# A hybrid attention and HGRN layer on one core: p·w_pp at the front, two column blocks in seven half-size products, their sums built during the first value columns

## The chip, the cores and the metric

The kernel runs on one core of a Trainium2 chip. The metric is the device time of one execution in microseconds (us); lower is better. TensorE (PE) does the matmuls, and PEld stands for its weight loads. VectorE (DVE), ScalarE (ACT) and GpSimd (POOL) work on tiles in the on-chip memories SBUF and PSUM. SyncE (SP) issues nearly all transfers, in the order in which they stand in its queue.

## The reference

x is 1024 tokens by 2048. What is computed, cut to the products that matter here:

```
u = rmsnorm(x, g_pre)
z = u @ w_in                   # 2048 x 9216; columns: attention q k v gate (1024 each),
                               # HGRN q, f_fwd, f_bwd, v, gate (1024 each)
y = [attention(q,k,v) * silu(gate) | rmsnorm(hgrn(q,f,v)) * silu(gate)]
h = x + rmsnorm(y @ w_out, g_post)          # 2048 x 2048
e = p @ w_pp                                # p 1024 x 256, w_pp 256 x 2048
out = h + rmsnorm(sigmoid(h @ w_pg) * e, g_ple)
```

All of it is float32.

## The kernel before

Each float32 product is made of three matmuls. The activations are split into a high part (fp32r) and a low part (bf16), the weights likewise: `uh` and `ul` hold the two parts of u transposed, for two halves of 512 tokens. A weight piece of 256 KB (`piece`, L69 to L85) is loaded as `raw` by SP; ACT casts it to `wh` (L82), POOL subtracts to get `wl` (L83), and DVE casts it to `wb` (L84). The matmuls are hi·wh, hi·wl and lo·wb. Each of the four kinds of tile has 3 buffers, so a piece's cast waits until the piece three back has been used. PSUM has 8 banks of 128x512: four with tag `gb`, four with tag `wk`.

The program goes through these stages; a scheduler orders the instructions of each engine.

1. `prenorm` (L155) loads x in eight tiles of 128 tokens (1 MB each), squares and scales them, transposes them on PE (`xp`, L171) and splits them into `uh` and `ul`. The first 512 attention value columns (`v_group(0, ...)`, L729) are computed in three passes over the 16 pieces of their weights: for tokens of tiles 0 and 1, of 2 and 3, and of 4 to 7, each as soon as those tiles are normalised. In a pass with two tiles a piece feeds 6 matmuls and every second `wl` is made by DVE; with four tiles it feeds 12.
2. `v_group(1)`, `(2)` and `(3)`: the other attention value columns (2560) and the HGRN value columns (7168, 7680), all eight token tiles at once, 24 matmuls of 512 columns for a piece.
3. Eight HGRN heads (`hgrn`, L229). Each has four products of 128 columns (`group`, L93: 96 matmuls of 512 columns): forward gate, backward gate, q, and the output gate (L376, columns 8192 on). The first `group` of the next head, and this head's own last one, are interleaved with the head's small matmuls: the scan's `pl` and `pa`, the state update `pu` (L366), the output `pout` (L385 to L389) and the last transposes `po` (L405).
4. Eight attention head pairs, then `y_phase` for either half of the tokens (y·w_out), then `g_phase(0)` and `g_phase(1)` (h·w_pg). p·w_pp is computed inside `g_phase` by `e_phase`, which uses `gemm` on the `wk` banks (tile `pe`, L810, L811, L814), for both halves 96 matmuls; its result goes to `G`, where the gate multiplies it.

Of the kernel before, what the change touches and what calls it, by code (L numbers as in the profile page):

```python
# [705 lines left out]
def tile_hybrid(ctx, tc, x, p, positions, w_in, w_out, g_pre, g_post, g_hg, lb_fwd, lb_bwd, w_pg, w_pp, g_ple, out):  # L706
# [22 lines left out]
    def v_group(cg, toks, pool):  # L729
        c0 = (2048, 2560, 7168, 7680)[cg]  # L730
        pb = {t: (K.gb() if t < NGB else K.wk("vb")) for t in toks}
        for k in range(KT):
            wh, wl, wb = K.piece(w_in[128 * k:128 * k + 128, c0:c0 + 512], [512], prio=False,
                                 sub=V if len(toks) == 2 and k % 2 else None)
            for t in toks:
                hi = K.uh[t // 4][:, k, 128 * (t % 4):128 * (t % 4) + 128]
                nc.tensor.matmul(pb[t], hi, wh, start=(k == 0), stop=False)  # L737
                nc.tensor.matmul(pb[t], hi, wl, start=False, stop=False)  # L738
            for t in toks:
                lo = K.ul[t // 4][:, k, 128 * (t % 4):128 * (t % 4) + 128]  # L740
                nc.tensor.matmul(pb[t], lo, wb, start=False, stop=(k == KT - 1))
        for t in toks:
            vo = pool.tile([128, 512], F32, name="vo", tag="vo", bufs=3)
            (nc.scalar.copy if t % 2 else V.tensor_copy)(vo, pb[t])
            nc.sync.dma_start(vD[cg][128 * t:128 * t + 128, :], vo)

    with tc.tile_pool(name="p0", bufs=1) as p0:
        warm = K.sp.tile([128, 1], F32, name="warm", bufs=1)
        V.memset(warm, 1.0)
        nc.scalar.activation(warm, warm, AF.Sqrt)  # L750
        K.prenorm(x2, g_pre, p0, (0, 1))
        v_group(0, (0, 1), p0)
        K.prenorm(x2, g_pre, p0, (2, 3))
        v_group(0, (2, 3), p0)
        late = K.prenorm(x2, g_pre, p0, (4, 5, 6, 7))
        v_group(0, (4, 5, 6, 7), p0)
        with tc.issue_after(late[0].ins), tc.issue_after(late[1].ins):
            K.hg_consts((lb_fwd, lb_bwd), g_hg)
        for cg in range(1, 4):
            v_group(cg, tuple(range(8)), p0)  # L760
    with tc.tile_pool(name="big", bufs=1) as big:
        K.big = big
        for h in range(8):
            K.hgrn(w_in, h, vD[2 + h // 4][:, 128 * (h % 4):128 * (h % 4) + 128], yD[8 + h])
            if h == 0:
                with tc.issue_after(late[0].ins), tc.issue_after(late[1].ins):
                    K.att_consts(positions)
        for hp in range(8):
            K.att(w_in, hp, vD[hp // 4][:, 128 * (hp % 4):128 * (hp % 4) + 128], yD[hp])
    fin = ctx.enter_context(tc.tile_pool(name="fin", bufs=1))  # L770
    Y = [fin.tile([128, 4, D], F32, name=f"Y{i}", tag=f"Y{i}") for i in range(2)]
    yss = [fin.tile([128, 4, 4], F32, name=f"yss{i}") for i in range(2)]
    gss = [fin.tile([128, 4, 4], F32, name=f"gss{i}") for i in range(2)]
    korder = list(range(8, 16)) + list(range(8))

    def s2(name):
        return fin.tile([128, 512], F32, name=name, tag="s2", bufs=3)

    def g2(src, cs):
# [161 lines left out]
    def every3(f, ext={}, off=0):  # L941
        def hook(cg, j, k=None):
# [3 lines left out]
            if n in ext:  # L946
                ext[n]()
# [80 lines left out]
```

## Time and profile before

| | us |
|---|---|
| median of 3 runs | 2906.36 (2903.96 to 2910.01) |
| the profiled execution | 2911.69 |
| its span, first to last instruction | 2909.9 |
| PE busy | 2785.7 (96%) |
| DVE busy | 1508.4 (52%) |
| POOL busy | 1023.8 (35%) |
| mean granted clock of TensorE | 0.992 |

The span is what the trace covers; 1.8 us of the profiled execution lie around it. A busy share is an average over stages that have different limits, so the stages are to be read one by one: where PE is busy through a stage, only fewer or shorter matmuls shorten it; where it isn't, some other engine or a transfer ends last there. The trace lacks some matmul records.

### The profile page before, as it was taken

The page shows a single profiled execution, that of the slowest core. Times are in us where ns is not written, and L with a number is a line of the kernel's source. Part 1 is how long each engine was busy: PE and PEld are TensorE (multiplying, and loading weights), DVE is VectorE, ACT ScalarE, POOL GpSimd, SP SyncE. Part 2 cuts the span into 40 slices and gives each one's busy share as a digit, 9 for nine tenths or more (in the row PEclk, how much of TensorE's full clock was granted, in tenths as well). Part 3 has the DMA queues.
Part 4 walks back from the last instruction along what each step waited for, and adds up shares of the span by engine and source line. Part 5 has one row for each costly group of instructions (what it writes and reads, how often), then busy time and mean ns, then how long its engine had stood idle before and what let it go on. Part 6 is the DMA issues. An engine that isn't in the chain of part 4 may idle for free. (4 is left out here: it accounts for less than half of the span.)

```text
span 2909.9 us, 46582 instructions
## 1 busy us (share of the span) xinstructions
PE 2785.7 (96%) x18128; PEld 1885.7 (65%) x18384; DVE 1508.4 (52%) x2833; ACT 925.5 (32%) x1672; POOL 1023.8 (35%) x769
## 2 busy tenths in 40 slices
PE   6999999999999999999999999999999899999997
PEld 4666666676667676676666666666566566665664
DVE  8601116856346346356655555555755645555555
ACT  5311112222122112124434444443533223333323
POOL 2422223413313313322222222222244554666555
PEclk9999999999999999999999999999999999999998
DMA  6412221211111111121221222122344543433453
GB/s 226 121 55 80 77 86 39 66 52 39 57 52 44 52 52 45 51 65 55 78 70 45 73 76 71 47 74 71 113 122 133 159 142 97 131 113 109 146 155 106
DMA packets 251614, 250.54 MB, mean 86 GB/s; under 512 B 21633, under 2 KB 175233, under 8 KB 250241
## 3 DMA queue, kind: packets, MB, share of 16 engines
q1 hardware_dynamic: 242224, 238.62, 27.6%
q10 hardware_dynamic: 9168, 8.93, 0.9%
q8 instruction: 144, 2.36, 0.3%
q14 instruction: 78, 0.63, 0.1%
HBM read 205.54 MB, written 29.36 MB: 81 GB/s over the span
## 5 line engine op out<-in xcount | busy, mean ns | idle before, releaser
L83 POOL TENSOR_TENSOR wl<-raw,wh 128x512 fp32r<-128x512 f32 x568 | 764.7, 1350 | 1599.8 <-ACT wh L82 1507.1
L84 DVE CAST wb<-raw 128x512 bf16<-128x512 f32 x584 | 430.5, 740 | 785.2 <-PE gb L106 281.8
L82 ACT CAST wh<-raw 128x512 fp32r<-128x512 f32 x584 | 358.4, 617 | 1241.7 <-PE gb L101 414.7
L101 PE MATMUL gb<-uh,wh 128*128 128x512 f32 x1792 | 744.3, 415 | 0.0
L102 PE MATMUL gb<-uh,wl 128*128 128x512 f32 x1792 | 708.6, 395 | 0.0
L106 PE MATMUL gb<-ul,wb 128*128 128x512 bf16 x1632 | 405.7, 380 | 9.8 <-issue 1.8
L101 PEld LDWEIGHTS gb<-uh,wh 128*128 128x128 f32 x1792 | 337.1, 188 | 82.9 <-issue 1.2
L102 PEld LDWEIGHTS gb<-uh,wl 128*128 128x128 f32 x1792 | 337.1, 188 | 68.9 <-issue 1.0
L106 PEld LDWEIGHTS <-wb 128*128 128x128 bf16 x1792 | 158.4, 98 | 204.6 <-issue 54.3
L810 PE MATMUL gb<-wh,yh 128*128 128x512 f32 x512 | 231.2, 452 | 2.8 <-DVE Y L842 2.8
L810 PE MATMUL gb<-wh,th 128*128 128x512 f32 x480 | 215.8, 450 | 0.0
L811 PE MATMUL gb<-wl,yh 128*128 128x512 f32 x512 | 203.7, 398 | 4.7 <-POOL wl L83 4.7
L811 PE MATMUL gb<-wl,th 128*128 128x512 f32 x480 | 190.6, 397 | 5.4 <-POOL wl L83 5.4
L645 DVE CUSTOM_DVE_ANT_1 asm<-asc,amask 128x512 f32<-128x512 f32 x128 | 88.3, 690 | 119.9 <-PE asc L639 119.7
L814 PE MATMUL gb<-wb,yl 128*128 128x512 bf16 x479 | 133.7, 383 | 1.6
L814 PE MATMUL gb<-wb,tl 128*128 128x512 bf16 x452 | 126.2, 384 | 1.0
L650 ACT ACTIVATE asm<-asm,anm 128x512 f32<-128x512 f32 x128 | 92.5, 722 | 90.3 <-DVE anm L648 90.0
L810 PEld LDWEIGHTS gb<-wh,yh 128*128 128x128 f32 x512 | 97.6, 191 | 33.3 <-DVE Y L842 3.3
L737 PE MATMUL gb<-wh,uh 128*128 128x512 f32 x256 | 116.4, 461 | 1.4 <-ACT wh L82 1.3
L811 PEld LDWEIGHTS gb<-wl,yh 128*128 128x128 f32 x512 | 97.4, 190 | 24.3 <-POOL wl L83 5.9
L738 PE MATMUL gb<-wl,uh 128*128 128x512 f32 x256 | 102.4, 407 | 10.9 <-POOL wl L83 7.9
L634 PE MATMUL asc<-ak,aqt 128*32 128x256 bf16 x1536 | 109.7, 401 | 3.2 <-issue 2.4
(274 smaller groups left out, 3668.4 us busy)
## 6 DMA issues: line engine op xcount, KB each, us to landing
raw<-in_w_in_dram SPq DMA_DIRECT2D x320, 256.0 KB
raw<-in_w_out_dram SPq DMA_DIRECT2D x128, 256.0 KB
raw<-in_w_pg_dram SPq DMA_DIRECT2D x128, 256.0 KB
xt<-in_x_dram SPq DMA_DIRECT2D x8, 1024.0 KB
vD<-vo SPq DMA_DIRECT2D x32, 256.0 KB
raw<-yD SPq DMA_DIRECT2D x32, 256.0 KB
xr<-in_x_dram SPq DMA_DIRECT2D x32, 256.0 KB
ak<-ak SPq DMA_DIRECT2D x96, 64.0 KB
```

Of the source, the lines that this page charges most:

```text
L82: nc.scalar.copy(wh, raw)
L83: (sub or nc.gpsimd).tensor_tensor(wl, raw, f32(wh), op=ALU.subtract)
L84: nc.vector.tensor_copy(wb, raw)
L101: nc.tensor.matmul(pb[hf], wh[:, k], self.uh[hf][:, kt], start=(kt == 0), stop=False)
L102: nc.tensor.matmul(pb[hf], wl[:, k], self.uh[hf][:, kt], start=False, stop=False)
L106: mm = nc.tensor.matmul(pb[hf], wb[:, k], self.ul[hf][:, kt], start=False, stop=(kt == KT - 1))
L634: t = nc.tensor.matmul(sc[32 * r:32 * r + 32, :256], qb[:, sq, 32 * r:32 * r + 32], KS[s][:, h, r::4], start=(s == 0), stop=False, skip_gr ...
L737: nc.tensor.matmul(pb[t], hi, wh, start=(k == 0), stop=False)
L738: nc.tensor.matmul(pb[t], hi, wl, start=False, stop=False)
L810: nc.tensor.matmul(pb[t], a, pc[0], start=first, stop=False)
L811: nc.tensor.matmul(pb[t], a, pc[1], start=False, stop=False)
L814: nc.tensor.matmul(pb[t], lo[:, k, 128 * t:128 * t + 128], pc[2], start=False, stop=last)
```

## The change

**p·w_pp.** `e_product(0)` and `e_product(1)` compute it at the head of the program, ahead of `prenorm`: per half 1 load of p, 8 transposes, 8 pieces of w_pp, 96 matmuls. The result leaves PSUM through 16 tiles `eo` a half and is stored to DRAM (`eD`, 32 transfers of 256 KB for both). `g_phase` loads it back (`e_load`, 4 transfers of 1 MB a half). The `e_phase` of the end and the hooks around it are gone. `xt` has 4 buffers in place of 5.

**Two column blocks.** The HGRN value columns (1024 of them) and the HGRN output gate of all heads (1024) are each computed by a `Block`: the 2048 rows and the 1024 columns of the weights are halved, the activations too, and the block takes seven products of half-size operands in place of eight. Each product has 8 pieces of 12 matmuls, so a block has 672 matmuls where `v_group(2)` and `(3)`, or the eight gate groups, had 768. Four of the weight operands are sums: T2, T1, T3 and T4 are formed by DVE from `raw`, `rb` and `TB` before they are split. Four of the activation operands are sums too, loaded from DRAM (`rh`, `rl`, 8 loads of both a block). The results are combined on ACT and DVE. The gate's are multiplied by their sigmoid and stored to `zD`, and each head loads its 512 KB into `hgt` in place of its fourth `group`.

**The activation sums.** `s_build`, called 8 times, makes four sums for each of 8 row tiles: 12 DVE instructions and 4 ACT casts a call, and 8 stores (`sh`, `sl`; 12.6 MB in all).

```diff
+    def e_product(hf, pool, stage):
+        src = pool.tile([128, 4, PLE], F32, name="pr", tag="pr", bufs=2)
+        nc.sync.dma_start(src, pin[512 * hf:512 * hf + 512, :].rearrange("(t p) c -> p t c", p=128))
...
+        for cg in range(4):
+            def sink(t, p):
+                eo = stage.tile([128, 512], F32, name="eo", tag="tA", bufs=4)
+                (V.tensor_copy if t % 2 else nc.scalar.copy)(eo, p)
+                nc.sync.dma_start(eD[hf][128 * t:128 * t + 128, chunk(cg)], eo)
+            gemm(w_pp, (eh, el), [0, 1], 512 * cg, sink, 2, K.gb)
...
+    def s_build(pool, kk):
...
+        add(x1, a21, l21)
+        add(x2, a22, l22)
+        add(x0, a11, l11)
+        add(x2, x1, x2)
+        s2 = x("sx3")
+        sub(s2, x2, x0)
+        sub(x1, x0, x1)
+        sub(x0, a12, s2)
+        add(x0, x0, l12)
+        for i, t in enumerate((x2, s2, x1, x0)):
...
+            nc.scalar.copy(h, t)
+            sub(l, t, f32(h))
+            nc.sync.dma_start(sD[i][0][:, kk], f32(h))
+            nc.sync.dma_start(sD[i][1][:, kk], l)
...
+        def weights(self, name, kk):
...
+            elif name == "T2":
+                t = self.raw(kk, 0, 1)
+                sub(t, t, self.raw(kk, 0, 0, True))
+                d = self.TB[:, kk]
+                sub(d, self.raw(kk, 1, 1, True), t)
+                t = d
+            elif name == "T1":
+                t = self.raw(kk, 1, 1)
+                sub(t, t, self.TB[:, kk])
+            elif name == "T3":
+                t = self.raw(kk, 1, 1)
+                sub(t, t, self.raw(kk, 0, 1, True))
...
+            nc.scalar.copy(wh, t)
+            sub(wl, t, f32(wh), nc.gpsimd)
+            V.tensor_copy(wb, t)
...
+        def run(self):
...
+            self.product(0, orig(0, 0), "11", True)
...
+            self.product(1, orig(0, 1), "21", True)
...
+            self.product(0, comb(1), "T2", False)
...
+            self.product(1, comb(0), "T1", True)
...
+            self.product(0, comb(2), "T3", False)
...
+            self.product(1, comb(3), "22", False)
...
+            self.product(0, orig(1, 1), "T4", False)
...
+            e_product(0, p0a, p0)
+            e_product(1, p0a, p0)
             K.prenorm(x2, g_pre, p0a, (0, 1))
...
+        v_group(1, tuple(range(8)), p0)
+        with tc.tile_pool(name="p0s", bufs=1) as p0s:
+            for kk in range(8):
+                s_build(p0s, kk)
...
+            Block((7168, 7680), False, v_out(2), p0, False).run()
+            Block((8192, 8704), True, z_out("hg", p0), p0, True).run()
...
-        self.group(w_in, base + 4096, lambda hf, p: self.gate_evac(gt[:, 512 * hf:512 * hf + 512], p))
+        nc.sync.dma_start(gt, self.zD["hg"][h])
...
     def g_phase(hf, G, hook, fin_t=None, get=None, tail=1):
+        e_load(hf, G)
         for cg in range(4):
-            if cg < 2:
-                e_phase(hf, G, 2 * cg)
-                e_phase(hf, G, 2 * cg + 1)
```

The scheduler places the new instructions. On SP, whose queue issues the loads, this is the start of the program (L75 is the load of a weight piece, L159 that of an x tile):

```order
+L75 DMA raw<-in_w_pp_dram 128x512 x3
+L769 DMA pr<-in_p_dram 128x4x256 x2
 L159 DMA xt<-in_x_dram 128x2048
+L75 DMA raw<-in_w_pp_dram 128x512 x3
 L162 DMA gpre<-in_g_pre_dram 128x2048
+L781 DMA eD_102<-eo 128x512 x2
 L159 DMA xt<-in_x_dram 128x2048
-L75 DMA raw<-in_w_in_dram 128x512 x3
-L159 DMA xt<-in_x_dram 128x2048 x2
-L75 DMA raw<-in_w_in_dram 128x512 x3
-L159 DMA xt<-in_x_dram 128x2048 x2
+L75 DMA raw<-in_w_pp_dram 128x512 x2
```

The first loads of w_pp and of p, and the first stores `eD`, now stand between the loads of x.

On DVE, in the third pass of `v_group(0)` (tokens 512 to 1023), the casts `wb` (L84) stood one behind the other before:

```order
L422 TENSOR_SCALAR am<-aj_3970 128x1
L465 SCALAR_TENSOR_TENSOR ainv<-am,ainv 128x1
L84 CAST wb<-raw 128x512 x13
L744 COPY vo<-vb 128x512 x2
L84 CAST wb<-raw 128x512 x16
L744 COPY vo<-gb 128x512 x2
```

Now four instructions of `s_build` (tiles `sx_...`, `sxl`; L808 is `add` and L811 is `sub` of the changed kernel) stand between one cast and the next, here for two casts in the middle of that pass:

```order
L84 CAST wb<-raw 128x512
L808 TENSOR_TENSOR sx_2363<-uh_94,ul_96 128x512
L808 TENSOR_TENSOR sx_2365<-sx_2364,sx_2365 128x512
L808 TENSOR_TENSOR sx_2400<-uh_95,ul_97 128x512
L811 TENSOR_TENSOR sx_2370<-sx_2365,sx_2363 128x512
L84 CAST wb<-raw 128x512
L811 TENSOR_TENSOR sx_2364<-sx_2363,sx_2364 128x512
L811 TENSOR_TENSOR sxl<-sx_2365,sxh 128x512
L811 TENSOR_TENSOR sx_2363<-uh_94,sx_2370 128x512
L811 TENSOR_TENSOR sxl<-sx_2370,sxh 128x512
L84 CAST wb<-raw 128x512
```

In all 61 of the 96 instructions of `s_build` stand in the third pass of `v_group(0)`, and 35 between the first five casts of `v_group(1)`.

On PE, within a head, this is what stood before between the last state update `pu` and the first output `pout` (29 matmuls of a `group`, L101, L102, L106; a few rows of them):

```order
L106 MATMUL gb<-ul_96,wb 128x512
L366 MATMUL pu<-hvt,hk_3699 128x128 x7
L106 LDWEIGHTS wb
L106 MATMUL gb<-ul_96,wb 128x512
...
L101 MATMUL gb<-uh_94,wh 128x512
L102 MATMUL gb<-uh_94,wl 128x512
...
L106 MATMUL gb<-ul_97,wb 128x512
L385 MATMUL pout<-hvt,ATT 128x128
L389 MATMUL pout<-hst,Q_3364 128x128
```

And now, with the same names:

```order
L106 MATMUL gb<-ul_96,wb 128x512
L366 MATMUL pu<-hvt,hk_6099 128x128 x7
L385 MATMUL pout<-hvt,ATT 128x128
L106 LDWEIGHTS wb
L106 MATMUL gb<-ul_96,wb 128x512
...
L106 MATMUL gb<-ul_97,wb 128x512
L101 MATMUL gb<-uh_94,wh 128x512
L102 MATMUL gb<-uh_94,wl 128x512
L385 MATMUL pout<-hvt,ATT 128x128
L387 MATMUL pout<-hst,Q_5764 128x128
```

Seven matmuls of a `group` (that of the next head's forward gate) stand between `pu` and the bulk of `pout` where 29 stood. Behind `pout`, ahead of `po`, 22 stand where 96 stood.

## Rows read from the trace of the kernel before

**Rows 1.** The page, its head and part 1: span, then busy time, share of the span and instructions of each engine.

```profile
span 2909.9 us, 46582 instructions
...
PE 2785.7 (96%) x18128; PEld 1885.7 (65%) x18384; DVE 1508.4 (52%) x2833; ACT 925.5 (32%) x1672; POOL 1023.8 (35%) x769
```

**Rows 2.** Busy time by stage, over the whole span. Columns: the stretch (us from the start), its length, busy us (and instructions) of PE, PEld, DVE, ACT and POOL, the granted clock, the mean busy share of the 16 DMA engines, GB/s. The stretches are: x and the first two passes of `v_group(0)`; its third pass; `v_group(1)` to `(3)`; the heads; then, behind the attention pairs and the two `y_phase` that are left out, `g_phase(0)` with `g_phase(1)` as far as the last `pe` matmul, and the rest of `g_phase(1)`.

```profile
0.00:98.40 98.40, 69.51 (x315) 44.93 (x320) 78.63 (x138) 55.13 (x94) 33.12 (x28) 0.97 0.61 206
98.40:141.90 43.50, 43.40 (x188) 28.64 (x191) 24.54 (x78) 11.90 (x21) 19.31 (x15) 1.00 0.38 92
141.90:401.40 259.50, 258.71 (x1135) 177.40 (x1154) 28.44 (x60) 36.27 (x60) 61.68 (x49) 1.00 0.24 70
401.40:1268.00 866.60, 836.17 (x7581) 601.59 (x7668) 462.37 (x902) 188.09 (x307) 256.63 (x197) 1.00 0.18 53
...
2457.40:2755.00 297.60, 279.88 (x1206) 179.81 (x1229) 166.85 (x207) 104.74 (x202) 180.14 (x132) 0.98 0.40 121
2755.00:2910.00 155.00, 135.21 (x564) 86.46 (x573) 84.87 (x123) 44.91 (x85) 86.85 (x62) 0.94 0.43 133
```

**Rows 3.** POOL in order of time, in the third pass of `v_group(0)` and then in `v_group(1)`. Columns here and in the other rows in order of time: start, us of the entry, engine, line, operation, out<-in, count, and in brackets the idle time before it with what ended it.

```profile
120.36 1.29 POOL L83 TENSOR_TENSOR wl<-raw,wh 128x512 fp32r<-128x512 f32 x1 [1.43 <-ACT wh L82]
123.09 1.29 POOL L83 TENSOR_TENSOR wl<-raw,wh 128x512 fp32r<-128x512 f32 x1 [1.43 <-ACT wh L82]
...
152.15 1.26 POOL L83 TENSOR_TENSOR wl<-raw,wh 128x512 fp32r<-128x512 f32 x1 [3.91 <-ACT wh L82]
157.54 1.26 POOL L83 TENSOR_TENSOR wl<-raw,wh 128x512 fp32r<-128x512 f32 x1 [4.13 <-ACT wh L82]
```

**Rows 4.** DVE in order of time: a cast `wb` in the third pass of `v_group(0)`, the end of that pass, and a cast in `v_group(1)`.

```profile
123.46 1.21 DVE L84 CAST wb<-raw 128x512 bf16<-128x512 f32 x1 [1.52 <-PE vb L738]
...
141.90 1.29 DVE L744 COPY vo<-vb 128x512 f32<-128x512 f32 x2 [0.87 <-PE vb L741]
...
153.38 0.43 DVE L84 CAST wb<-raw 128x512 bf16<-128x512 f32 x1 [4.86 <-PE vb L741]
```

**Rows 5.** The front. DVE's first scaling of an x tile; PE's first transposes and its first product.

```profile
9.06 2.35 DVE L167 SCALAR_TENSOR_TENSOR xt<-xt,xr,gpre 128x2048 f32<-128x2048 f32 x1
...
11.56 3.65 PE L171 MATMUL xp<-ident,xt 128*128 128x128 f32 x16 [11.56 <-DVE xt L167]
16.49 0.79 PE L737 MATMUL gb<-wh,uh 128*128 128x512 f32 x1 [1.28 <-ACT wh L82]
```

**Rows 6.** What the transfers reach: columns as in group 2, for three 5 us pieces of the front, one stretch at the start of the heads and one of `g_phase(1)`.

```profile
5.00:10.00 5.00, 0.00 (x0) 0.00 (x0) 1.89 (x7) 2.21 (x3) 0.00 (x0) 1.00 0.98 415
20.00:25.00 5.00, 3.86 (x24) 2.72 (x23) 3.65 (x6) 3.15 (x6) 0.00 (x0) 1.00 0.87 298
30.00:35.00 5.00, 3.28 (x18) 2.02 (x16) 4.69 (x12) 4.47 (x9) 1.68 (x2) 1.00 0.94 313
402.00:410.00 8.00, 7.95 (x36) 5.84 (x36) 1.91 (x4) 2.38 (x4) 1.27 (x1) 1.00 0.78 270
2700.00:2735.00 35.00, 34.89 (x153) 23.24 (x155) 18.51 (x18) 8.03 (x13) 16.50 (x13) 1.00 0.51 159
```

**Rows 7.** DVE and POOL in order of time within a head: DVE's product of two SBUF tiles (`Q`, two of 128x512 in an entry) without and with POOL's `wl` beside it, and that `wl`.

```profile
693.08 1.29 DVE L281 TENSOR_TENSOR Q<-Q,TB 128x512 f32<-128x512 f32 x2
...
698.70 2.03 DVE L281 TENSOR_TENSOR Q<-Q,TB 128x512 f32<-128x512 f32 x2
...
697.64 1.94 POOL L83 TENSOR_TENSOR wl<-raw,wh 128x512 fp32r<-128x512 f32 x1 [6.37 <-ACT wh L82]
```

**Rows 8.** The end of a head, in order of time: PE's last `pu` entry, the first and last `pout`, and `po`; then DVE's last state update `hst` and the normalised output `hon`.

```profile
712.58 1.83 PE L366 MATMUL pu<-hvt,hk 128*128 128x128 f32 x14 [1.12 <-DVE hk L352]
...
720.74 0.38 PE L385 MATMUL pout<-hvt,ATT 128*128 128x128 f32 x2
...
725.42 0.39 PE L387 MATMUL pout<-hst,Q 128*128 128x128 f32 x2
...
747.22 1.04 PE L405 MATMUL po<-ident,hon 128*128 128x128 f32 x8
...
715.87 1.49 DVE L372 SCALAR_TENSOR_TENSOR hst<-hst,TB,pu 128x128 f32<-128x128 f32 x4
...
729.71 1.29 DVE L398 TENSOR_TENSOR hon<-pout,hr 128x512 f32<-128x512 f32 x2
```

**Rows 9.** The `pe` work (p·w_pp) at the end. First PE in the four stretches that hold it: length, PE busy, clock, DMA share, GB/s, of which the first, the third and the sum are shown. Then the first of the three matmuls of the tile `pe` (count, ns min/median/max, first and last start), and two PE entries in order of time with the wait before them.

```profile
2457.40:2472.00 14.60, 13.43 (x56) 1.00 0.25 74
...
2678.00:2697.00 19.00, 14.84 (x55) 0.91 0.47 139
...
sum 64.00, PE 53.95; mean PE 13.49
...
L810 PE MATMUL pe<-wh,eh x64: 388/584/988, 2457.5 to 2753.5; 128*128 128x512 f32 x64
...
2690.16 0.71 PE L810 MATMUL pe<-wh,eh 128*128 128x512 f32 x1 [3.18 <-DVE G L900]
...
2750.11 0.50 PE L810 MATMUL pe<-wh,eh 128*128 128x512 f32 x1 [1.91 <-DVE G L900]
```

**Rows 10.** DVE's last scalings, two SBUF tiles in, beside POOL's work at the end (count, ns min/median/max).

```profile
L990 DVE SCALAR_TENSOR_TENSOR G<-G,gr,Y x12: 746/1248/1792, 2882.5 to 2904.3; 128x512 f32<-128x512 f32 x12
```

More of the change, by code (lines that the diff above doesn't have):

```diff
@@ L727, in tile_hybrid @@
     vD = [K.dr.tile([S, 512], F32, name=f"vD{i}") for i in range(4)]
[L729 to L779, printed above, removed]
-        t = fin.tile([128, 512], F32, name="g2", tag="g2", bufs=2)
-        nc.sync.dma_start(t, src[0:1, cs].to_broadcast([128, 512]))
-        return t
@@ new lines, in v_group @@
+    def v_group(cg, toks, pool):
+        c0 = (2048, 2560, 7168, 7680)[cg]
+        pb = {t: (K.gb() if t < NGB else K.wk("vb")) for t in toks}
+        for k in range(KT):
+            wh, wl, wb = K.piece(w_in[128 * k:128 * k + 128, c0:c0 + 512], [512], prio=False,
+                                 sub=V if len(toks) == 2 and k % 2 else None)
+            for t in toks:
+                hi = K.uh[t // 4][:, k, 128 * (t % 4):128 * (t % 4) + 128]
+                nc.tensor.matmul(pb[t], hi, wh, start=(k == 0), stop=False)
+                nc.tensor.matmul(pb[t], hi, wl, start=False, stop=False)
+            for t in toks:
+                lo = K.ul[t // 4][:, k, 128 * (t % 4):128 * (t % 4) + 128]
+                nc.tensor.matmul(pb[t], lo, wb, start=False, stop=(k == KT - 1))
+        for t in toks:
+            vo = pool.tile([128, 512], F32, name="vo", tag="tA", bufs=4)
+            (nc.scalar.copy if t % 2 else V.tensor_copy)(vo, pb[t])
+            nc.sync.dma_start(vD[cg][128 * t:128 * t + 128, :], vo)
@@ new lines, in tile_hybrid @@
+    K.zD = zD
+    with tc.tile_pool(name="big", bufs=1) as big:
+        K.big = big
+        for h in range(8):
+            K.hgrn(w_in, h, vD[2 + h // 4][:, 128 * (h % 4):128 * (h % 4) + 128], yD[8 + h])
+            if h == 0:
+                with tc.issue_after(late[0].ins), tc.issue_after(late[1].ins):
+                    K.att_consts(positions)
+        for hp in range(8):
+            K.att(w_in, hp, vD[hp // 4][:, 128 * (hp % 4):128 * (hp % 4) + 128], yD[hp])
+    fin = ctx.enter_context(tc.tile_pool(name="fin", bufs=1))
@@ L945, in hook @@
                 f(n // 3)
[L946 to L955 removed]
+        return hook
+    y_phase(1, every3(lambda u: h_unit(0, u, r0_)))
     hT[1] = half_tiles("t", 1)
```

195 lines of the change are left out of this document (161 added, 34 removed).

## The prediction

> **What bounds the kernel now.** The first page part to read is the busy time of the engines: PE is busy for 2785.7 of 2909.9 us [rows 1]. So most of the time can only fall with the number of matmuls. Next come the stages [rows 2], to see where that holds. In the third pass of the first value columns PE is busy for 43.40 of 43.50 us and in the value groups for 258.71 of 259.50. In the first 98.40 us it is busy for 69.51 alone while DVE has 78.63 and the DMA engines 0.61 of their time: PE waits there for x. The heads leave 30 us in 866.60 idle, the stretch with the `pe` work at the end 18 in 297.60.
>
> What a piece costs PE is read from the distance of POOL's subtractions where nothing else limits: 123.09 − 120.36 = 2.73 us for 12 matmuls, 157.54 − 152.15 = 5.39 for 24 [rows 3], which is 0.2246 us a matmul. In these 2.73 us POOL works 1.29. DVE's cast takes 0.43 us by itself and 1.21 when it starts inside that subtraction [rows 4], and ends just behind it: the two exclude each other. In the heads the same is seen from POOL's side: `wl` takes 1.94 us, and two products of SBUF tiles on DVE 2.03 us in place of 1.29 [rows 7].
>
> **The change, part by part**, against the profiled 2911.7 us.
>
> *p·w_pp at the end goes.* Its four stretches last 64.0 us [rows 9]. They hold 192 `pe` matmuls and about 27 others (217 entries in the four, of which some 190 are `pe`), 27·0.2246 = 6 us. The stall of 3.18 us at 2690.16 and of 1.91 at 2750.11 [rows 9] are in it: `wk` banks wait for DVE's copies. With its transposes I put **−60**; at least the matmuls go, 192·0.2246 = 43 and the two stalls, −48; at most −64. In its place come 8 loads of 1 MB. Those of the second half stand on SP behind a release of `h0`, with five pieces of `g_phase(1)` ahead of them, and the stretch moved 121 GB/s on average [rows 2], so 8.4 MB fit in time; but 4.2 MB at 415 GB/s are 10 us in which the weight pieces share the queues. I take **+3** (0 to 12).
>
> *p·w_pp at the front comes.* x's first product stands at 16.49 us [rows 5]. p needs no scaling (2.35 us) and no square, so I estimate the first `e` matmul at 8. Then 16 pieces of 2.73 = 43.7. A column group has two pieces and the third set of weight tiles comes free only near its end, about 0.8 us late, 8 times: 6. With the transposes PE is through at about 60. The transfers agree: w_pp 4.2, p 1.0, five of x and `gpre` 6.2, `eD` 8.4, together some 19 MB, at 298 to 313 GB/s [rows 6] about 62 us. Behind it x's passes 1 and 2 are bound by DVE: 78.6 us, less four scalings of 2.35 and some 3 us of small work that were done beside `e`, about 65. The third pass so starts at 125 in place of 98.4: **+27**. If more of DVE's work on x fits beside `e`, +15; if DVE can do none of it there (SP's queue puts eD stores, which wait for the copies, ahead of x's loads), 60 + 78 − 98 = +40.
>
> *The sums.* 61 instructions of `s_build` stand between the 16 casts of the third pass. DVE's product of two SBUF tiles has a pitch of 0.60 to 0.65 us alone [rows 7]. DVE then has 61·0.60 + 16·0.35 + 4.2 (the last splits of x) = 46.4 us, PE 46.2 with what precedes the pass. That alone would cost nothing. But POOL's 16·1.28 = 20.5 us cannot lie beside them, since both kinds of instruction shut POOL out [rows 4, 7]: 46.4 + 20.5 = 67, so +21. In `v_group(1)` 35 of them stand in five pieces: 21 + 2 + 6 + 5 for copies and gaps = 34 against 27, +7. Some 6 us come back, as three buffers of pieces run ahead. **+22** (5 to 45). The Trainium skill, page "SBUF — State Buffer", section "Who interferes with whom", says that a DVE instruction with two SBUF inputs contends with POOL's reads and that the loser blocks for the whole instruction, not merely slows. The trace agrees: 0.43 became 1.21 us, behind a `wl` of 1.29. By that rule the sums cost these 22 us, without it about 0 to 5.
>
> *The two blocks.* The value block replaces 32 pieces of 5.39 = 172.5 us by 56 of 2.73 = 152.7; the gate block replaces as many matmuls. −19.8 each, **−39.6**. What is against it are transfers: the seven products take 2 KB rows at 256 KB a piece, T2 three for each piece. In T2's 8·2.73 = 21.8 us: 24 pieces, 6.3 MB, at about 300 GB/s 21.0 us, and 1.6 MB of sums at x's 415 another 3.8: 24.8, +3. DVE and POOL exclude each other too: 2·0.60 + 0.35 + 1.28 = 2.83 us for a piece against 2.73, +1. **+8** for both blocks (0 to 30, the upper end by 270 GB/s [rows 6] over T2 and T3 and casts that come late). The Trainium skill, page "DMA: Bandwidth & Descriptors", section "Where 436 GB/s comes from", puts the limit of transfers between HBM and one core at about 358 GB/s. No row agrees: x came in at 415 [rows 6], and weight pieces beside x at 298. By that figure T2's 7.9 MB would take an estimated 22 us and the block lose next to nothing.
>
> *The heads lose filler.* Their fourth group was interleaved with the tail of the head. The last `pu` ends at 714.4; DVE's states `hst`, which `pout` needs, at 717.36; `pout` came at 720.74 [rows 8], so nothing waited. Now seven matmuls stand there, 1.6 us: PE waits 717.4 − 716.0 = 1.4. From the end of `pout` (725.8) to `hon` (731.0) are 5.2 us [rows 8]; 22 matmuls cover 4.9: 0.3. Eight heads at 1.7: **+13.6** (0 to 24, the upper end if each chain slips by as much again).
>
> Sum: −60 + 3 + 27 + 22 − 39.6 + 8 + 13.6 = −26. 2911.7 − 26 = 2886 in a profiled execution; that one is 5.3 us above the median of before, so 2880 as a median.
>
> **The rivals.** Less than 0.2% (5.8 us) cannot be told from no change.
>
> (a) *The sums cost twice as much.* DVE's instructions with two SBUF inputs beside POOL's work took up to 1.79 us and 1.25 in the median at the end [rows 10]. At 0.80 each, 61·0.2 + 35·0.2 = 19 us more; the gain falls to about 7 and the time is 2900, no change. For it: they stand in the cast's own queue, so PE's next piece is held. Against it: alone they take 0.65.
>
> (b) *Transfers bound the blocks*, and it is slower. From T2 to the product 22 a block loads 14.7 MB of weights and, with the first ring loaded ahead, 11 MB of sums, and stores 1 MB: 26.7 MB in 87 us is 306 GB/s. That is within 298 to 313 of the front [rows 6], so it is close; weight pieces reached 159 GB/s at a share of 0.51 [rows 6], 312 in proportion. At 230 GB/s each block would take 116 us there, +29 and not +4: 2880 + 50 = 2930. It decides from about 245 GB/s on downwards.
>
> (c) *The covers hold.* x's normalisation runs beside `e` (+15), POOL's subtractions find gaps (+5), the heads' waits stay below 1 us: 12 + 17 + 7 us less, about 2844. For it: PE's share in the front is low, and DVE's work on x needs only that x be there.
>
> (d) *The end doesn't give its 60 us*, as the read-back loads sit behind the `h0` release and the first gate product of `g_phase(1)` waits for `G` and holds its PSUM bank: 10 to 20 us, so 2895.
>
> **How the numbers follow.** The forecast within ±18 us has 0.46, (d) 0.08, (a) 0.14, (b) 0.12, (c) 0.20. Faster are the forecast, (c), (d) and a share of (a): 0.77; the same, most of (a) and the edge of (b): 0.11; slower, (b): 0.12. The range from 2843 to 2912 leaves out half of (b) and of what lies beyond (c). The forecast's own is 2862 to 2898.
>
> **What would show it.** In the changed profile the third pass should start at about 125 us with 61 sums on DVE and take about 65 us; a gap at T2 with DVE or a load of `rb` as releaser; `pout` waiting some 1.4 us for `hst` in each head; the two `g_phase` shorter by 29 and 35 us, less 3. The forecast is wrong if PE waits for `raw` throughout a block, if POOL's `wl` in the third pass is late by more than 2.5 us a piece, or if the stretch in front of the third pass doesn't grow.

## The result: 0.2% slower, and the profile after

The changed kernel takes 2915.13 us (median of 12 runs, 2910.11 to 2917.12), the kernel before 2908.39 beside it: a ratio of 1.0021, 95% interval 1.0012 to 1.003. Forecast were 2880 us, in a range of 2843 to 2912. So it is slower where a gain was forecast, just behind the range's upper end. The profiled execution has a span of 2913.3 us against 2909.9.

The page's head and part 1 of the changed kernel (against [rows 1]):

```profile
span 2913.3 us, 47353 instructions
...
PE 2761.8 (95%) x17933; PEld 1857.2 (64%) x18192; DVE 1703.8 (58%) x3061; ACT 981.7 (34%) x1772; POOL 1153.0 (40%) x833
```

PE is busy for 24 us less than before and the span is 3.4 us longer: 27 us more in which it is idle. The two blocks have 192 matmuls less, which at 0.2246 us each would be some 43 us. So by this estimate 19 of the 43 us went to matmuls that ran at the lower clock (below), and the 27 of idle time outweigh the rest. The same stages as in [rows 2], of the changed kernel; the columns are those of group 2. The stretches: p·w_pp at the front up to the first product of a value column; the first two passes; the third, as far as the first copy `vo` of its results; `v_group(1)`; the value block; the gate block; the heads, up to the first score of the attention; the two `g_phase`.

```profile
0.00:72.70 72.70, 53.65 (x237) 34.24 (x241) 48.98 (x81) 36.09 (x64) 29.04 (x26) 1.00 0.81 274
72.70:145.90 73.20, 62.34 (x286) 38.82 (x289) 57.50 (x100) 39.88 (x71) 27.67 (x18) 0.95 0.61 187
145.90:206.50 60.60, 50.56 (x197) 32.45 (x200) 55.55 (x80) 21.43 (x39) 33.19 (x16) 0.92 0.63 191
206.50:293.20 86.70, 85.71 (x370) 58.48 (x377) 42.31 (x114) 20.33 (x36) 34.27 (x18) 0.98 0.56 193
293.20:450.50 157.30, 154.63 (x661) 102.30 (x673) 86.75 (x112) 41.61 (x72) 75.21 (x56) 0.99 0.72 245
450.50:616.90 166.40, 157.87 (x661) 102.84 (x673) 98.43 (x111) 49.72 (x84) 93.94 (x68) 0.98 0.58 194
616.90:1386.30 769.40, 727.64 (x7089) 526.41 (x7173) 470.14 (x905) 175.92 (x289) 245.56 (x183) 0.99 0.20 59
2513.00:2913.00 400.00, 367.28 (x1575) 236.84 (x1604) 217.31 (x294) 130.64 (x251) 247.31 (x178) 0.97 0.45 140
```

Set against the same places of before this is the ledger, in us, with the last stretch to the end of the span. "Forecast" is the term of the prediction. A gate group of before is 96 matmuls of 0.2246 us, 21.56 us; the eight are taken out of the 929.0 us that the heads lasted.

| stretch | before | after | difference | forecast |
|---|---|---|---|---|
| start to the third pass | 98.3 | 145.9 | +47.6 | +27 |
| third pass and `v_group(1)` | 130.1 | 147.3 | +17.2 | +22 |
| value block (two groups of 86.5) | 173.0 | 157.3 | -15.7 | -15.8 |
| gate block (8 gate groups of 21.56) | 172.5 | 166.4 | -6.1 | -15.8 |
| heads without their gate groups | 756.5 | 769.4 | +12.9 | +13.6 |
| attention and `y_phase` | 1127.1 | 1126.7 | -0.4 | 0 |
| the two `g_phase` | 452.4 | 400.3 | -52.1 | -57 |

Three terms have the size that was forecast: the sums, the value block, the heads. Whether for the reason that was forecast is read below. The front is 20.6 us above its term, the gate block 10, the end gives 5 less.

**The front.** PE was busy for 69.5 of 98.4 us before [rows 2], so 29 us idle. Now it is busy for 53.65 + 62.34 = 116.0 of 145.9: 30 us idle. The stretch has grown by just what PE got to do. Where the idle time lies is told by PE's waits, added up. Before, 11.6 us stood ahead of its first transpose, 4.2 were waits for a tile of x, and 12.8 were waits for weight pieces (`wh`, `wl`, `wb`). So the prediction's reading that PE waits there for x holds for the smaller part of what follows the start. Two of the ten waits for pieces, from the kernel before, PE in order of time, with the wait and its releaser in brackets:

```profile
68.70 1.12 PE L738 MATMUL gb<-wl,uh 128*128 128x512 f32 x2 [2.13 <-POOL wl L83]
...
79.29 0.80 PE L738 MATMUL gb<-wl,uh 128*128 128x512 f32 x1 [2.56 <-POOL wl L83]
```

Now 9.3 us stand ahead of the first transpose, 9.5 are waits while p·w_pp is computed, and in the two passes 1.4 are for x and 8.9 for weight pieces. Four of the waits while p·w_pp is computed, in the changed kernel:

```profile
20.29 0.50 PE L742 MATMUL gb<-wl,eh 128*128 128x512 f32 x1 [1.73 <-POOL wl L83]
...
38.63 0.50 PE L741 MATMUL gb<-wh,eh 128*128 128x512 f32 x1 [1.93 <-ACT eo L780]
...
42.29 0.51 PE L741 MATMUL gb<-wh,eh 128*128 128x512 f32 x1 [2.02 <-ACT eh L150]
...
52.17 0.50 PE L742 MATMUL gb<-wl,eh 128*128 128x512 f32 x1 [1.75 <-POOL wl L83]
```

They are the weights' subtraction on POOL, the copy of a result (whose `eo` tile waited for its store), and the split of p's second half.

**What a wait costs behind it.** PE around three waits of the changed kernel; each wait's row, then the granted clock of the stretches of 5 us that hold it and that follow (columns: length, PE busy, clock, DMA share, GB/s).

```profile
99.54 1.22 PE L793 MATMUL gb<-wl,uh 128*128 128x512 f32 x2 [2.24 <-DVE wl L83]
...
171.55 0.79 PE L793 MATMUL vb<-wl,uh 128*128 128x512 f32 x1 [3.28 <-POOL wl L83]
...
187.29 0.51 PE L793 MATMUL vb<-wl,uh 128*128 128x512 f32 x1 [4.56 <-POOL wl L83]
```

```profile
95.00:100.00 5.00, 1.57 (x5) 0.89 0.15 49
100.00:105.00 5.00, 5.00 (x13) 0.50 0.53 157
105.00:110.00 5.00, 5.00 (x25) 0.93 0.32 71
...
170.00:175.00 5.00, 3.45 (x8) 0.56 0.44 135
175.00:180.00 5.00, 5.00 (x17) 0.76 0.81 233
...
185.00:190.00 5.00, 2.71 (x7) 0.76 0.29 84
190.00:195.00 5.00, 5.00 (x21) 0.89 1.01 338
```

The wait of 2.24 us at 99.5, with one of 1.20 for `wh` just ahead of it (a stretch in which PE was busy for 1.57 of 5 us), is followed by 5 us at a granted clock of 0.50, the lower of the two levels, 1.2 GHz, throughout. Behind the wait of 3.28 us at 171.5 the clock is 0.56 and 0.76, behind that of 4.56 at 187.3 0.76 and 0.89. PE works on through these stretches, at half its speed for part of them. Over the whole span the mean clock is 0.986 against 0.992: 2913.3·0.014 - 2909.9·0.008 = 17.5 us more of missing clock, which agrees with the 19 us above. No term of the prediction held this.

**The sums** in the third pass, DVE and then POOL in order of time:

```profile
168.49 0.68 DVE L808 TENSOR_TENSOR sx<-sx,ul 128x512 f32<-128x512 f32 x1
...
170.35 1.69 DVE L811 TENSOR_TENSOR sxl<-sx,sxh 128x512 bf16<-128x512 f32 x1
171.97 1.50 DVE L84 CAST wb<-raw 128x512 bf16<-128x512 f32 x1
173.38 1.76 DVE L808 TENSOR_TENSOR sx<-uh,ul 128x512 f32<-128x512 f32 x1
```

```profile
167.72 6.88 POOL L83 TENSOR_TENSOR wl<-raw,wh 128x512 fp32r<-128x512 f32 x3 [4.58 <-ACT wh L82]
```

Alone the sums take 0.68 us. Where POOL works, one takes 1.69 or 1.76 and the cast 1.50; POOL's three `wl` take 6.88 us, 2.29 each in place of 1.29 [rows 3]. That is the exclusion the prediction counted on. The Trainium skill's rule (page "SBUF — State Buffer", section "Who interferes with whom": the loser blocks for the whole instruction) agrees as far as the rows go: a sum of 0.68 us becomes 1.7, 1.0 us more beside a `wl` of 1.29.

Besides the waits of 3.28 and 4.56 us for `wl` there is a third, behind the pass's last product, of PE in order of time:

```profile
207.10 0.50 PE L792 MATMUL vb<-wh,uh 128*128 128x512 f32 x1 [2.69 <-ACT vo L799]
```

PE waits there for a bank, whose copy `vo` on ACT stands behind casts of the sums, which wait for DVE. The three waits are 10.5 us; the rest of the 17 is the clock behind them.

**The transfers** did not hold the blocks. T2 of the value block (columns of group 2):

```profile
336.80:358.50 21.70, 21.70 (x98) 14.55 (x97) 19.81 (x25) 5.03 (x9) 11.57 (x8) 1.00 0.90 312
```

T2 moved 312 GB/s and lasted 21.7 us, its matmul time; PE was busy throughout. Rival (b) is out: T2's 24.8 us, forecast from 300 GB/s, were 21.7; 312 GB/s over them are 6.8 MB, so 1.1 of the 7.9 MB had come before it began. The +3 us that the forecast had for T2's transfers are not there: the value block's 157.3 us are 154.6 of busy PE and 2.7 idle, of which the trace names 1.6 as waits for `wl`. In the gate block T2 waits, and for POOL. First the longest of PE's waits over that block (us in all, times, longest), then POOL and DVE in order of time while its T2 begins:

```profile
PE vb L894 <- POOL wl L811: 4.7, 4, 2.1
```

```profile
502.68 3.42 POOL L971 TENSOR_TENSOR tA<-tA,zsg 128x512 f32<-128x512 f32 x2
506.06 4.82 POOL L811 TENSOR_TENSOR wl<-TB,wh 128x512 fp32r<-128x512 f32 x3
```

```profile
501.50 3.46 DVE L811 TENSOR_TENSOR raw<-raw,rb 128x512 f32<-128x512 f32 x2
504.88 3.43 DVE L811 TENSOR_TENSOR TB<-rb,raw 128x512 f32<-128x512 f32 x2
```

POOL's products of the gate with its sigmoid (L971, 1.3 to 1.7 us each) stand among the subtractions of T2, and DVE's two sums of a piece take 1.7 us each beside them, not 0.68.

**The heads.** From the first `po` of a head to that of the next there are 100.4, 85.5, 86.9, 86.8, 86.8, 86.8 and 87.2 us. Before there were 108.3 to 109.0, which less a gate group of 21.56 is 86.8 to 87.4. So the heads from the third on lose nothing by their missing filler, and the 12 us lie in the second head alone. PE's waits over the eight heads hold none at `pout`, and one at `po`. POOL and then PE in the second head, in order of time, with the first `po` of the third head as the last row; then the granted clock of one stretch of it (columns as above):

```profile
759.36 6.90 POOL L334 TENSOR_TENSOR TB<-F 128x1024 f32<-128x1024 f32 x1 [5.13 <-DVE F L241]
```

```profile
773.10 0.80 PE L102 MATMUL gb<-uh,wl 128*128 128x512 f32 x1 [4.04 <-POOL wl L83]
...
780.90 0.66 PE L275 MATMUL pl<-hq,KD 128*32 128x32 f32 x32 [4.02 <-DVE hq L226]
...
824.93 0.66 PE L405 MATMUL po<-ident,hon 128*128 128x128 f32 x4 [1.37 <-DVE hon L398]
...
910.39 1.10 PE L405 MATMUL po<-ident,hon 128*128 128x128 f32 x8
```

```profile
775.00:780.00 5.00, 1.88 (x5) 0.50 0.20 52
```

POOL's `TB` takes 6.90 us here, 2.58 in the median of the heads. Beside it DVE makes the attention's angles (`aang`, two SBUF tiles in), which in the kernel before were through at 552 us, ahead of the second head's `TB` at 559.5 (3.96 us). `wl` stands behind `TB`, so PE waits for it, then for `hq`; from 770 to 785 the granted clock is 0.63, 0.50 and 0.50, which is 6.9 us of missing clock. Every run with the two blocks has it: the second head takes 100.0 to 100.9 us in each of the others but one (gate_in_heads, 103.2), and 108.3 in e_front_only, which has no blocks, as before. No run moves the angles, so that they are the cause is read from the rows and not tested.

### The profile page after: what moved, and what is told of

Its sections match the earlier page's. It is cut to its first block, busy times and chain, and to the rows that moved or that the text cites. A ratio compares the mean times of both kernels' runs of the same rounds, so it can differ in the third digit from the quotient of the medians.

```text
span 2913.3 us, 47353 instructions
## 1 busy us (share of the span) xinstructions
PE 2761.8 (95%) x17933; PEld 1857.2 (64%) x18192; DVE 1703.8 (58%) x3061; ACT 981.7 (34%) x1772; POOL 1153.0 (40%) x833
## 5 line engine op out<-in xcount | busy, mean ns | idle before, releaser
L83 POOL TENSOR_TENSOR wl<-raw,wh 128x512 fp32r<-128x512 f32 x504 | 717.9, 1429 | 1318.1 <-ACT wh L82 1244.6
L84 DVE CAST wb<-raw 128x512 bf16<-128x512 f32 x520 | 393.0, 761 | 482.7 <-PE gb L106 202.3
L101 PE MATMUL gb<-uh,wh 128*128 128x512 f32 x1536 | 641.9, 418 | 0.0
L102 PE MATMUL gb<-uh,wl 128*128 128x512 f32 x1536 | 610.5, 397 | 4.0 <-POOL wl L83 4.0
L82 ACT CAST wh<-raw 128x512 fp32r<-128x512 f32 x520 | 318.8, 618 | 850.5 <-PE gb L101 326.3
L106 PE MATMUL gb<-ul,wb 128*128 128x512 bf16 x1384 | 345.3, 380 | 9.3 <-issue 1.6
L101 PEld LDWEIGHTS gb<-uh,wh 128*128 128x128 f32 x1536 | 290.0, 189 | 71.0 <-issue 1.2
L102 PEld LDWEIGHTS gb<-uh,wl 128*128 128x128 f32 x1536 | 290.0, 189 | 63.4 <-POOL wl L83 4.5
L106 PEld LDWEIGHTS <-wb 128*128 128x128 bf16 x1536 | 135.6, 98 | 172.9 <-issue 46.3
L811 POOL TENSOR_TENSOR wl<-raw,wh 128x512 fp32r<-128x512 f32 x96 | 129.5, 1355 | 140.5 <-ACT wh L880 137.1
L880 ACT CAST wh<-raw 128x512 fp32r<-128x512 f32 x96 | 59.4, 620 | 193.7 <-DVE raw L811 75.0
L882 DVE CAST wb<-raw 128x512 bf16<-128x512 f32 x96 | 77.7, 818 | 71.2 <-DMA raw<-in_w_in_dram 25.8
```

The lines of the kernel that those rows point to most:

```text
L82: nc.scalar.copy(wh, raw)
L83: (sub or nc.gpsimd).tensor_tensor(wl, raw, f32(wh), op=ALU.subtract)
L84: nc.vector.tensor_copy(wb, raw)
L101: nc.tensor.matmul(pb[hf], wh[:, k], self.uh[hf][:, kt], start=(kt == 0), stop=False)
L102: nc.tensor.matmul(pb[hf], wl[:, k], self.uh[hf][:, kt], start=False, stop=False)
L106: mm = nc.tensor.matmul(pb[hf], wb[:, k], self.ul[hf][:, kt], start=False, stop=(kt == KT - 1))
```

## The experiments

Each is an edit of the changed kernel. The first number is the median; the ratio is that to the kernel before, measured beside it (medians of 2906.6 to 2907.6). The changed kernel's 2915.1 stood beside 2908.4, so differences from it are good to about 1 us.

### One part alone

e_front_only takes out the sums and blocks:

```diff
-            for kk in range(8):
-                s_build(p0s, kk)
...
-            Block((7168, 7680), False, v_out(2), p0, False).run()
-            Block((8192, 8704), True, z_out("hg", p0), p0, True).run()
+        for cg in range(2, 4):
+            v_group(cg, tuple(range(8)), p0)
```

> The changed kernel with p·w_pp at the front, but without the activation sums and the two blocks: HGRN value columns and gate groups as before. Theory 1 (the front was mis-sized and nothing of it comes from the sums): the third pass of the first value columns starts at about 146 us as in the changed kernel (98 before) and takes 44 us; the end gives back 52 us; the whole is 2908 + 47 - 52 = 2903, about 0.2% below before. Rival (the loads and sums of the blocks reach into the front and delay x): the third pass starts at about 125 and the whole is 2883.

2908.04 us, ratio 1.0006 (0.9997 to 1.0015), 5 above the 2903 expected. Its third pass starts at 147.9 us and takes 43.6. So the 47 us are p·w_pp's own, and nothing of the blocks reaches into the front; what the end gave back is used up there.

blocks_only takes out `e_product` ahead and puts `e_phase` back:

> The changed kernel with p·w_pp at the end as before, but with the sums and the two blocks. Theory 1: third pass from 98 us on, about 61 long (+17), second value columns +6, value block -17, gate block with the heads +1: 2908 + 7 = 2915, slower by 0.2%. Rival (the blocks pay as forecast, and only their lying behind a late front cost time): 2908 + 4 = 2912 or less.

2911.50, ratio 1.0016 (1.0007 to 1.0026): the third pass starts at 97.7 and takes 62. The whole is what the rival had; the stages are those of theory 1, but for the gate block, which takes 161.6 us here. The blocks with their sums and the heads lose some 4 us by themselves.

e_behind moves the two calls behind `v_group(1)`:

> p·w_pp moved from the front to behind the second value group, ahead of the first block, where x is no longer loaded; all else as in the changed kernel. Theory 1 (in the front p·w_pp costs 47 us because its stores, loads and casts stand in x's way): third pass from 98 us on, p·w_pp takes its matmul time of 16 pieces, 44 to 48 us, so the whole is that of the changed kernel within 4 us, 2911 to 2916: the front hides nothing of it. Rival (x's normalisation and p·w_pp overlap well in the front, and the rest was lost elsewhere): 15 to 20 us slower than the changed kernel, 2932.

2923.77, ratio 1.006 (1.0045 to 1.0075): 9 us above the changed kernel, between the two. There p·w_pp takes 53.6 us, not 44 to 48 (columns of group 2; one of the seven waits of PE in it):

```profile
248.00:301.60 53.60, 48.15 (x202) 30.05 (x206) 25.57 (x38) 19.83 (x40) 20.45 (x14) 0.97 0.69 236
```

```profile
257.03 0.51 PE L742 MATMUL gb<-wl,eh 128*128 128x512 f32 x1 [0.74 <-POOL wl L83]
```

It waits some 0.74 us in six of its eight column groups by itself, each time for `wl` (a column group has only two pieces), and the clock is 0.97. So the front, where it adds 47.6, hides 6 us of it (9 by the medians). The forecast had it hide some 25 of 52.

### What holds the front

```diff
# e_light
-                (V.tensor_copy if t % 2 else nc.scalar.copy)(eo, p)
+                nc.scalar.copy(eo, p)
-            gemm(w_pp, (eh, el), [0, 1], 512 * cg, sink, 2, K.gb)
+            gemm(w_pp, (eh, el), [0, 1], 512 * cg, sink, 2, K.gb, wsub=V)
# e_no_store
-                nc.sync.dma_start(eD[hf][128 * t:128 * t + 128, chunk(cg)], eo)
# pass_wl
-                                 sub=V if len(toks) == 2 and k % 2 else None)
+                                 sub=V if len(toks) == 2 else None)
# x_first
-            e_product(0, p0a, p0)
-            e_product(1, p0a, p0)
             K.prenorm(x2, g_pre, p0a, (0, 1))
+            e_product(0, p0a, p0)
             v_group(0, (0, 1), p0)
             K.prenorm(x2, g_pre, p0a, (2, 3))
+            e_product(1, p0a, p0)
# front_no_scale
-            nc.vector.scalar_tensor_tensor(xt, xt, r, self.gpre, op0=ALU.mult, op1=ALU.mult)
```

> The changed kernel with two edits of p·w_pp at the front: all copies of its results out of PSUM on ACT (half were on DVE), and its 16 subtractions wl on DVE in place of POOL. Theory 2 (the front is bound by DVE and POOL together, since they exclude each other; p·w_pp adds 16 casts of 0.43, 16 wl of 1.28, 16 copies of 0.68 and 8 splits of 0.42 there, 42 us, which is what it cost): 11 us of copies and 16·(1.28 - 0.68) = 10 less, so the third pass starts at about 126 to 132 in place of 146 and the whole is 2895 to 2902. Rival (transfers: x's loads behind the stores in SP's queue, or the bandwidth): third pass at 143 to 149, the whole 2912 to 2918.

2907.23, 0.9992 (0.9982 to 1.0002). Third pass at 140.1: 6 us earlier, not 14 to 20.

> The changed kernel without the 32 stores of p·w_pp's result; g_phase loads rows of x in its place, as many bytes, so what is left out are 8.4 MB of stores, and the output is another. Theory 2: DVE's and POOL's work in the front is the same, the third pass starts at 140 to 146 and the whole is 2909 to 2915. Rival (transfers): p·w_pp's copies no longer wait for a store, x's loads move up in SP's queue, 8.4 MB less at 300 GB/s are 28 us less: third pass at 118 to 130, the whole 2887 to 2900.

2908.81, 1.0004 (0.9994 to 1.0013). Third pass at 142.1: 4 us. With 8.4 MB less the DMA share of its first 69 us was 0.48, where the changed kernel has 0.81 in its first 72.7, and it made 4 us.

> The changed kernel with all 32 subtractions wl of the first two passes of the first value columns on DVE (16 of them were on POOL). Theory 2 (DVE and POOL together are what the two passes last on: POOL's wl took 1.61 us on average in the front, DVE's 0.68): 16 us less of the two, so the passes last 60 to 66 us in place of 73, the whole is 2902 to 2908. Rival (DVE alone is the bound): DVE has 11 us more, the passes last 80 to 84, the whole 2922.

2908.74, 1.0001 (0.9991 to 1.001). Third pass at 139.8: 6 us, all in the two passes (67 us in place of 73.2).

> The changed kernel with another order in the front: the first two x tiles, then the first half of p·w_pp, the first pass, the next two x tiles, the second half of p·w_pp, the second pass. The work is the same. Theory 2 (the work of DVE and POOL bounds the front whatever the order): third pass at 138 to 146 us, the whole 2908 to 2915. Rival (x is late because it stands behind p·w_pp in the queues, and PE idles for it later): third pass at 118 to 130, the whole 2887 to 2900.

2923.35, 1.0054 (1.0039 to 1.007). Third pass at 155.7, 10 us later: both expectations fell. Its p·w_pp starts at 30.2 us, behind the transposes of two x tiles; PE's wait for the second:

```profile
24.78 3.65 PE L171 MATMUL xp<-ident,xt 128*128 128x128 f32 x16 [6.32 <-DVE xm L117]
```

p·w_pp first at least fills the start, where x isn't ready.

Then the question was whether DVE's work holds the front at all.

> The changed kernel without the eight scalings of x (2.35 us each on DVE, 18.8 us): x is split as it is, and the output is another. Theory 2 (DVE's work and POOL's hold the front): third pass at 126 to 134 us in place of 146, first pass of the value columns earlier by 8 or more. Rival (the front lasts as long as PE's own matmuls and the start-up, and DVE's time is hidden): 142 to 146.

2908.50, 1.0007 (0.9996 to 1.0018). Third pass at 144.3, so within the rival's 142 to 146, and theory 2 falls in its strong form. The front of this kernel (columns of group 2):

```profile
0.00:71.50 71.50, 55.34 (x236) 35.01 (x237) 36.12 (x71) 32.94 (x59) 23.66 (x26) 0.98 0.80 269
71.50:144.30 72.80, 63.04 (x296) 39.84 (x294) 52.02 (x101) 42.79 (x75) 25.58 (x18) 0.95 0.64 206
```

DVE has 88 us of work in 144 and the front is as long as before. Not DVE's total bounds it, but PE's own work (118 us here) with the waits for single pieces.

> The changed kernel with the edits of e_no_store, e_light and pass_wl together (the output is another, as p·w_pp's result isn't stored). Alone they brought the third pass from 146 forward by 4, 6 and 6. If they are different waits: 130, the whole 2897 to 2900. If one wait takes the place of another: 136 to 140.

2899.83, 0.9972 (0.9958 to 0.9986). Third pass at 133.8, 12 us of 16, between the two expectations:

```profile
0.00:62.70 62.70, 52.81 (x225) 33.62 (x225) 34.35 (x75) 40.37 (x75) 1.00 (x9) 0.97 0.54 185
62.70:133.60 70.90, 61.88 (x306) 40.92 (x304) 61.53 (x121) 42.79 (x76) 2.75 (x3) 0.95 0.60 192
```

POOL has next to nothing there, and PE still takes 114.7 us of 133.6, at a clock of 0.97 and 0.95. Of the 18.9 us in which it is idle 7.1 stand ahead of its first transpose, 2.8 are two waits in p·w_pp, and 9.0 are waits in the passes: 4.2 for `wh` on ACT, 2.2 for `wl` on DVE, 2.6 for x.

### What holds the sums and the blocks

```diff
# sums_spread (the casts of v_group(1) are kept in K.wbs)
+        with tc.issue_after(K.wbs[2 * kk].ins):
+            add(x1, a21, l21)
...
+            with tc.issue_after(K.wbs[2 * kk + 1].ins):
+                sub(l, t, f32(h))
# wl_dve
-                                 sub=V if len(toks) == 2 and k % 2 else None)
+                                 sub=V if (len(toks) == 2 and k % 2) or len(toks) == 4 else None)
# gate_in_heads (in z_out; the same two lines stand in hgrn behind the load of hgt)
-            nc.scalar.activation(sg, t, AF.Sigmoid)
-            nc.gpsimd.tensor_tensor(t, t, sg, op=ALU.mult)
```

> The changed kernel with the same sums, but none in the third pass: the DVE instructions of each of the eight calls may issue only behind two casts of the second value group, about six to a piece. Theory (DVE and POOL exclude each other, so the sums cost what the sum of both exceeds PE's time of a piece: 6·0.60 + 0.43 + 1.26 = 5.3 us against 5.39): third pass 44 to 46 us in place of 61, second value group 86 to 92: 15 to 22 us faster than the changed kernel, 2895 to 2900. Rival (the sums cost PE time wherever they stand, since they delay the casts): no faster than the changed kernel, 2911 to 2916.

2904.70, 0.9995 (0.9986 to 1.0005), 10 us below the changed kernel. Third pass, `v_group(1)` and value block (columns of group 2):

```profile
146.30:191.50 45.20, 45.10 (x197) 29.96 (x200) 29.32 (x84) 13.06 (x23) 20.44 (x16) 1.00 0.39 99
191.50:277.00 85.50, 84.86 (x374) 58.14 (x379) 73.22 (x110) 28.19 (x51) 24.66 (x17) 1.00 0.63 209
277.00:436.80 159.80, 154.01 (x662) 101.54 (x673) 80.53 (x112) 41.96 (x72) 74.77 (x57) 1.00 0.80 278
```

The third pass takes 45.2 us and `v_group(1)` 85.5: the sums cost nothing there, with DVE busy for 73 of 85.5 us. Of the 17 us some go back to the value block, 159.8: PE waits in it at 291 to 299 us, for weights, after a stretch in which the DMA engines were full (a share of 1.00 from 279 to 291 us, at 382 GB/s, as the value group's stores `vD` and the block's loads of sums and weights meet).

> The changed kernel with the 16 subtractions wl of the third pass on DVE (0.68 us each) in place of POOL (1.28). Theory (DVE and POOL exclude each other): DVE's and POOL's sum in the third pass falls by 16·0.6 = 10 us, the pass lasts 51 in place of 61 and the whole is 2905. Rival (DVE alone is the bound there): DVE gets 11 us more, the pass lasts 65 to 72 and the whole is 2920 or more.

2907.62, 1.0000 (0.999 to 1.001). The third pass takes 45.5 us, 15 less; but `v_group(1)` takes 97.2, 10 more: the scheduler put 48 sums between the casts of the pass in place of 61, and 48 in place of 35 between those behind it. That fewer sums stood there is part of the 15, so this run alone doesn't separate the exclusion from the order; the rows of DVE and POOL above do.

> The changed kernel with the gate's sigmoid and its 16 products with it taken out of the second block and done in the heads (ACT and POOL, on the loaded tile). Theory (POOL's 16 products of 1.29 us shut out the block's weight casts, so the second block takes 166 us where the first takes 157): second block about 157, the heads the same, 8 to 10 us faster than the changed kernel, 2906. Rival (the second block is slow because its loads or its position are): 2913 to 2917.

2921.02, 1.0043 (1.0028 to 1.0058). The gate block takes 156.5 us, 10 less, as the theory has it (in the other runs that leave it as it was it takes 161.6 to 166.9); but the heads take 784.9 in place of 769.4, from the third head on 1.8 us more for each. The 16 products cost more in the heads than in the block: the expectation that they would be hidden there was wrong.

### Versions that beat both

spread_light is sums_spread, e_light and pass_wl together. spread_light_blk adds, in the blocks:

```diff
-            sub(wl, t, f32(wh), nc.gpsimd)
+            sub(wl, t, f32(wh))
...
-            nc.gpsimd.tensor_tensor(t, t, sg, op=ALU.mult)
+            V.tensor_tensor(t, t, sg, op=ALU.mult)
```

> Edits of sums_spread, e_light and pass_wl together: sums only behind the casts of the second value group, copies of p·w_pp on ACT, its wl and those of the first two passes on DVE. If the three act on different stretches: -10 of the first, -6 to -8 of the second, -8 of the third: 2889 to 2893, 0.6% below before. If they share one bound, so that each gives back what the other gains: 2900 to 2905.

2893.98, 0.995 (0.9933 to 0.9966): 21 us below the changed kernel, where the three alone gave 10, 8 and 6, and 1 us above the range that was expected if they act on different stretches. They nearly do. The sums act apart from the other two, but in the front e_light and pass_wl, which bring the third pass forward by 6 us each alone, bring it forward by 8 together (137.6).

> spread_light and in both blocks wl on DVE in place of POOL, with the 16 products of gate and sigmoid on DVE too. Theory (the second block lasts 166 us against 157 because POOL's products and wl shut out the casts; a piece has 2·0.6 + 0.35 + 0.6 = 2.15 us of DVE then against 2.83 of both): blocks 153 to 156 each, 10 to 14 us below spread_light. Rival (loads bound the blocks): 0 to 3 us below spread_light.

2883.71, 0.9911 (0.9892 to 0.993). Its value block and gate block (columns of group 2):

```profile
265.50:423.70 158.20, 153.91 (x675) 101.46 (x673) 89.82 (x168) 41.73 (x72) 0.00 (x0) 1.00 0.82 282
423.70:579.20 155.50, 153.59 (x675) 101.69 (x673) 97.83 (x177) 49.81 (x84) 2.66 (x3) 1.00 0.62 206
```

POOL is empty, and the blocks take 158.2 and 155.5 us, against 163.4 and 162.7 in spread_light. So DVE alone, busy for 57 to 63% of the time, is better than DVE and POOL in turn.

## Why the prediction was wrong

- **The front** is the step that failed, 20.6 us. It said: p·w_pp is through at 60, and behind it "x's passes 1 and 2 are bound by DVE: ... about 65". The first product of a value column came at 72.7: p·w_pp started at 10.9, not 8, and took 60 us, not 52, with 9.5 us of waits where 6 were counted and the transposes of a tile of x in it. The passes took 73.2. DVE doesn't bound them: it is busy for 57.5 of the 73.2 us and PE for 62.3, and when the scalings were taken out altogether (front_no_scale) the front moved by 1.6 us. The bound came from DVE's busy time of 78.6 us before, which isn't work alone: an instruction on 128x1 that takes 0.16 us by itself took 1.23 there beside POOL's `wl`. What the runs show in its place is a sum: PE's own 116 us, and 30 in which it is idle, 9.3 at the start and nearly all the rest waits of 0.2 to 2.3 us, 13.5 in all for weight pieces. Of the 30 the stores make 4, POOL's and DVE's share in p·w_pp 6, POOL's in the passes 6, and the three together 12. Of the 18 that are left, the rows of front_three above name what PE waits for; no run takes these away.
- **Idle time was taken for room.** The 29 us in which PE idled before were read as waits for x, and so as a cover for p·w_pp. Only 4.2 of them were, behind the start; 12.8 were waits for weight pieces, and p·w_pp needs such pieces too. e_behind prices it: 53.6 us where it stands alone, 47.6 in the front.
- **The gate block**, 10 us: the prediction named the products on POOL nowhere in its sum, and the same price for both blocks. gate_in_heads shows them: without the products it takes 156.5 us.
- **The clock**, 17.5 us more of it missing, was in no term. It lies inside the others: (1 - 0.95)·73.2 = 3.7 us in the passes, 0.08·60.6 = 4.8 in the third pass, which without it would have cost 12, and 6.9 in the second head.
- **The end** gave 52 of 57. PE is busy there for 47.8 us less and idle for 4.7 less. Against the 60 of the prediction 8 came back, not 3; how much of that is the read-back isn't shown, as no wait of PE there names `G`, and the waits for POOL's `wl` are 9.8 us in place of 5.4.
- **Right by luck**: the heads and the value block. The heads cost 12.9 us where 13.6 were forecast, but not 1.7 us in each by waits for `hst` and `hon`: the third to the eighth lose nothing, and the second loses it all, in waits for `wl` and `hq` that no term named. The value block comes out to 0.1 us, but T2's 3 us are not in it, and in the runs that leave it as it was it lasts from 154.6 to 163.4 us.
- **Right**: the sums in the main (17 of 22), by DVE and POOL shutting each other out in the third pass, and at no cost beside other casts; but the +7 of `v_group(1)` was 0 (86.7 against 86.6), and part of the 17 is the clock. Also that transfers would not bound the blocks, against rival (b), which gave the right sign for the wrong reason. Rival (a), the sums at twice their cost, is out too.

## What to carry to other kernels

A stretch in which PE idles is no room for more work on PE if the idle is made of many short waits in the chain that feeds it: work that feeds through the same chain brings its own waits along. So see first what each wait is for, and forecast the work at the price that it has where it stands alone, unless a trace shows the overlap. Before work on two engines that exclude each other is added up as two, look whether the longer of the two instructions can be moved to the other engine: 0.68 us on DVE replaced 1.29 on POOL and its blocking here. And let the helper's instructions stand where the pieces are long (5.39 us), not where they are short (2.73): the same 96 sums cost 17 us in the one place and none in the other.
